# A 16x16 substitution joined by small matmuls, grouped beta/alpha matmuls, and a planner with other costs, in a two-layer hybrid DeltaNet step

## The chip, the core and the metric

The kernel runs on one core of a Trainium2 chip. The metric is the device time in microseconds (us) from start to end of one execution. TensorE (PE in the rows), VectorE (DVE), ScalarE (ACT), GpSimd (POOL) and the DMA queue of SyncE (SP) work side by side. Each works through its own instructions in the program's order, and semaphores tie them together.

## What is computed

128 context tokens and 256 latent tokens (384 in all) pass through two layers. What matters of one layer in the reference:

```python
hn = _rmsnorm(x, norm_g) * (1.0 + scale) + shift
proj = hn @ w_in                 # conv branch, q, k, v, z, beta, alpha, gates
beta = jax.nn.sigmoid(beta_l)    # 16 columns: 8 heads x 2 directions
g = -jnp.exp(a_log) * jax.nn.softplus(alpha_l + dt_bias)
# per head, direction and block of tokens (gated delta rule):
a = jnp.einsum('bhnid,bhnjd->bhnij', kb, k) * decay
a = jnp.where(strict, a, 0.0) + jnp.eye(CHUNK)
u = triangular_solve(a, v * beta)          # unit triangle
w = triangular_solve(a, kb * exp(g))
...
x = x + gate * (merged @ w_o)
```

The triangular solves need the inverse of a unit triangular matrix for each head, direction and block. A head has two directions and three blocks of 128 tokens, so six matrices of 128x128; there are 8 heads in each of 2 layers, 16 heads in all.

## The kernel before

Channels lie on the 128 partitions and the 384 tokens on the free axis. Each weight half of 512 KB comes by a DMA from SP, is rounded by ACT into `whi`, and the rest `wlo` is made by DVE (a few by POOL). An fp32 product is then three matmuls of 384 columns: `whi` with both parts of the activation pair, `wlo` with its first part (`mm3`). A *job* is 48 such matmuls that make one output tile of 128 channels; it runs as four *steps* of 12 (`slot`). In the rows `pm`, `pg` and `px` are PSUM tiles, `t` and `h` are tiles of the pools behind `t1`, `t2` and `h1`.

The order in which instructions are written is made by a planner in the Python code. Each emitted instruction is booked on a clock of its engine (`book`, with costs from `mm_`, `act`, `vec`, `dma`). Side work is written as generators (`spawn`): a `yield` asks to go on after the next step, a `yield "p"` asks to go on when the TensorE clock has passed the time at which the operands are booked. After every step `fill` writes pieces of the 31-tap convolution (`conv31`, on DVE, read from `px`) until the DVE clock has caught up with TensorE's.

In each layer 40 jobs make the conv branch inputs and k, q and v of the heads, five jobs a head. Then come the z jobs, the gates, the merges and the output projection. The heads' side work runs beside these 40 jobs and a dozen after them.

`invert` makes the inverse of a head's six matrices. It takes the 32x32 diagonal blocks (24 of them), sends them through DRAM (`dd`) so that each block lies on one partition of `ax`, and substitutes row by row on POOL: for each of 31 columns an outer product `o` and a subtraction. The result goes through DRAM (`dx`) back to `xc` on 128 partitions. Then small matmuls join 32x32 blocks to 64x64 (`ypf`, `ypb`, then `xf`, `xb`) and 64x64 to 128x128 (`y2p`, `x2p`). `head_out` uses the inverse `U` and runs the scan.

`ba_mm` makes beta and alpha: for each of 16 input tiles one fp32 matmul of 32 output channels and 384 columns, written to the PSUM partitions `32*(k%4)` on. In layer 0 these stand among the matmuls of the modulation (`mod_job`, operand `csil`), in layer 1 between the first steps.

Of the kernel before, what the change touches and what calls it, by code (L numbers as in the profile page):

```python
# [52 lines left out]
for _n, _w in PAR:  # L53
# [3 lines left out]

CST = [("ident", 128), ("mask_f", 128), ("mask_b", 128), ("xmask", 64),
       ("ones", 128), ("sel32", 32), ("sel2", 2)]
# [9 lines left out]
def hybrid_step_kernel(ctx: ExitStack, tc: tile.TileContext, x_in, cvec, w_mod, w_modt, w_first, w_in, w_ba,  # L69
# [63 lines left out]
    def act(out, in_, func, **k):  # L133
# [3 lines left out]
        return nc.scalar.activation(out, in_, func, **k)  # L137

    def mm_(out, lhsT, rhs, start, stop):
# [281 lines left out]
    def mod_job(l, cs):  # L421
# [21 lines left out]
        def finish(v):  # L443
# [14 lines left out]
            while "v" not in rs_x:  # L458
                yield
            h = make_hn(l, k)  # L460
            live[0] += 1 - (k % 2)
            yield "p"
            ba_mm(k, h)
            hn_done.add(k)
# [163 lines left out]
    def make_hn(l, k, lo_eng=ptt):  # L628
# [11 lines left out]
        split(hn[k], h, False, lo_eng)  # L640
        return h
# [171 lines left out]
    def invert(l, hd):  # L813
# [8 lines left out]
        yield  # L822
        dd = dram.tile([P, NI, 32], F32, tag="dd", name="dd", bufs=2)
        dma(out=dd, in_=dg.rearrange("p d b i -> p (d b) i"))
        yield 2
        ax = sub.tile([4 * NI, 32, 32], F32, tag="ax", name="ax", bufs=NA)
        for q in range(4):
            dma(out=ax[NI * q:NI * q + NI], in_=dd[32 * q:32 * q + 32].rearrange("j n i -> n j i"))
        pset(out=ax.rearrange("p i j -> p (i j)")[:, 0:1024:33], value=1.0)
        for j in range(31):  # L830
            n, m = 31 - j, j + 1
            o = sub.tile([4 * NI, 256], F32, tag="o", name="o", bufs=1)
            ov = o[:, 0:n * m].rearrange("p (r c) -> p r c", r=n)
            ptt(out=ov, in0=ax[:, j, j + 1:32].unsqueeze(2).to_broadcast([4 * NI, n, m]),
                                    in1=ax[:, j, 0:m].unsqueeze(1).to_broadcast([4 * NI, n, m]), op=ALU.mult)
            ptt(out=ax[:, j + 1:32, 0:m], in0=ax[:, j + 1:32, 0:m], in1=ov, op=ALU.subtract)
        dx = dram.tile([4 * NI, 32, 32], F32, tag="dx", name="dx", bufs=2)
        dma(out=dx, in_=ax, q="pool")
# [10 lines left out]
        vset(out=U[1][0:64, :, 64:128], value=0.0)  # L849
        xc = t1([P, NI, 32])  # L850
        for q in range(4):
            dma(out=xc[32 * q:32 * q + 32], in_=dx[NI * q:NI * q + NI].rearrange("n i c -> i n c"))
        yield 2
        x64, xt64 = h1([P, NI, 64]), h1([P, NI, 64])
        tt(out=x64.rearrange("p n (e c) -> p n e c", e=2), in0=xc.unsqueeze(2).to_broadcast([P, NI, 2, 32]),
           in1=C("xmask").rearrange("p (e c) -> p e c", e=2).unsqueeze(1).to_broadcast([P, NI, 2, 32]), op=ALU.mult)
# [169 lines left out]
    def layer(l):  # L1026
# [246 lines left out]

        hk = {}

        def open_layer():
            del rs_x["v"]
            yield from rows_task()
            for a in range(HNA):
                hk[a] = make_hn(l, a, tt)  # L1280
            st["open"] = True


        def first_half(i):
            def run(hs, at):
                if i == 0:
                    st["acc"] = [pm(), pm(), pm(), pg([P, NTOK])]
                for q in range(2):
# [3 lines left out]
                    else:  # L1292
                        settle(lambda: "open" in st)
                        if k + HNA < KT:
                            hk[k + HNA] = make_hn(l, k + HNA)

                    def mms(k=k, q=q, h=hk.pop(k) if l else None):
                        if l:
                            ba_mm(k, h)
                        for n in range(4):  # L1300
                            mm3(st["acc"][n], hs[0], 4 * q + n, hn[k], k == 0, k == KT - 1)
# [225 lines left out]
def _consts():  # L1527
# [9 lines left out]
    q, e, cc = i[:, None] // 32, np.arange(64)[None] // 32, np.arange(64)[None] % 32  # L1537
    put("xmask", (e == q % 2) & (cc <= i[:, None] % 32))
    put("mask_f", np.where(i[:, None] <= i[None, :], 0.0, NEG))
# [91 lines left out]
```

## Time and profile before

| what | before |
|---|---|
| median of 3 runs | 2449.17 us (2448.19 to 2454.17) |
| the profiled execution | 2447.77 us, span of its instructions 2446.0 us |
| PE busy | 2330.2 us (95%) |
| DVE busy | 1835.7 us (75%) |
| ACT busy | 951.6 us (39%) |
| POOL busy | 869.1 us (36%) |
| granted TensorE clock, mean | 0.984 |

A share is an average over stages. Matmuls are pipelined, so a row's mean duration of one matmul is longer than the distance between two starts; the distance between starts is what a matmul costs.

### The profile page before, as it was taken

The numbers are of one execution on the slowest core, as the hardware profiler recorded it, in microseconds if no ns is written. First come the engines' busy times: TensorE is split into PE (matmuls) and PEld (weight loads), VectorE is DVE, ScalarE is ACT, GpSimd is POOL, SyncE is SP. The second block draws the span as 40 slices with busy tenths as digits, with TensorE's granted clock in tenths as the row PEclk, the third lists the DMA queues.
The fourth block names the chain that finished last, engine by engine and source line by source line (L and its number), as shares of the span: only waits on it lengthen the run. The fifth ranks groups of instructions, "written<-read, shape, count | busy, mean of one in ns | idle before, by whom it ended". The sixth has DMA issues, their size and how long they took to land.

```text
span 2446.0 us, 40033 instructions
## 1 busy us (share of the span) xinstructions
PE 2330.2 (95%) x14727; PEld 2237.6 (91%) x14727; DVE 1835.7 (75%) x4223; ACT 951.6 (39%) x1823; POOL 869.1 (36%) x1192
## 2 busy tenths in 40 slices
PE   6999989989989999999999999999989999999997
PEld 4789988989979999999998998988889999999997
DVE  3447989989875599899977999999975489333533
ACT  4224444444454222223344444444454322222432
POOL 1120688667630111111242188756670011110212
PEclk9999999999999999999999999999999999999998
DMA  9874433333323688787853433333333477333443
GB/s 340 287 257 149 137 107 99 111 104 104 98 91 109 206 269 265 255 266 259 310 160 104 130 114 108 108 104 113 95 103 114 152 254 239 130 125 132 137 158 111
DMA packets 163269, 398.26 MB, mean 163 GB/s; under 512 B 40960, under 2 KB 70752, under 8 KB 163072
## 3 DMA queue, kind: packets, MB, share of 16 engines
q1 hardware_dynamic: 159376, 387.66, 48.9%
q0 software_dynamic: 2176, 5.90, 0.7%
q8 instruction: 116, 1.90, 0.3%
q10 hardware_dynamic: 1520, 2.13, 0.2%
q14 instruction: 81, 0.66, 0.1%
HBM read 379.72 MB, written 15.91 MB: 162 GB/s over the span
## 4 chain that ended last, share of the span: by engine, by line
PE 64%; DVE 19%; POOL 7%; DMA 3%; issue 3%; ACT 3%; SPq 1%; DVEq 0%; ACTq 0%; POOLq 0%
PE pm L148 54%; DVE t L177 10%; PE pg L148 8%; DVE wlo L177 4%; POOL ax L177 4%; POOL o L177 3%; ACT t L137 2%; DVE h L177 1%; DMA t<-in_w_mod_dram 1%; PE px L148 1%; ACT jk L137 1%; DVE rk0t L177 1%; PE pg L152 1%; SPq L201 1%; DMA w<-in_w_in_dram 1%
## 5 line engine op out<-in xcount | busy, mean ns | idle before, releaser
L148 PE MATMUL pm<-t,whi 128*128 128x384 f32 x7264 | 1903.6, 343 | 5.8 <-ACT whi L137 5.8
L148 PEld LDWEIGHTS pm<-t,whi 128*128 128x128 f32 x7264 | 1314.5, 190 | 26.8 <-ACT whi L137 7.4
L148 PE MATMUL pm<-t,wlo 128*128 128x384 f32 x3632 | 1232.6, 339 | 31.1 <-DVE wlo L177 31.1
L177 DVE TENSOR_TENSOR wlo<-w,whi 128x1024 fp32r<-128x1024 f32 x453 | 587.5, 1298 | 207.3 <-ACT whi L137 206.2
L148 PEld LDWEIGHTS pm<-t,wlo 128*128 128x128 f32 x3632 | 688.2, 189 | 38.1 <-DVE wlo L177 37.9
L137 ACT ACTIVATE whi<-w 128x1024 fp32r<-128x1024 f32 x480 | 505.2, 1054 | 383.0 <-PE pm L148 301.1
L177 POOL TENSOR_TENSOR ax<-ax,o 24x31 f32<-24x31 f32 (+15 forms) x496 | 332.4, 670 | 38.9
L137 ACT ACTIVATE t<-t 128x384 f32<-128x384 f32 (+5 forms) x299 | 137.7, 467 | 525.4 <-DVE t L177 479.9
L177 POOL TENSOR_TENSOR o<-ax 24x31 f32<-24x31 f32 (+15 forms) x496 | 309.4, 624 | 38.9
L177 DVE SCALAR_TENSOR_TENSOR t<-px,par,t 128x113 f32<-128x113 f32 (+26 forms) x768 | 248.7, 367 | 12.0 <-ACT px L137 6.9
L177 POOL TENSOR_TENSOR t<-t,t 128x384 fp32r<-128x384 f32 (+2 forms) x66 | 88.0, 1337 | 383.0 <-DVE t L177 305.4
L177 POOL TENSOR_TENSOR wlo<-w,whi 128x1024 fp32r<-128x1024 f32 x27 | 65.0, 2408 | 433.0 <-ACT whi L137 421.1
L177 DVE SCALAR_TENSOR_TENSOR px<-wm,pg 128x512 f32<-128x512 f32 x256 | 177.1, 692 | 8.7 <-DMA wm<-in_w_modt_dram 5.3
L177 DVE SCALAR_TENSOR_TENSOR wm<-wm,pg 128x512 f32<-128x512 f32 x256 | 167.2, 681 | 7.3 <-PE pg L152 7.3
L137 ACT ACTIVATE t<-pm 128x384 f32<-128x384 f32 x122 | 56.1, 488 | 176.1 <-PE pm L148 175.9
L148 PE MATMUL pg<-t,whi 128*128 128x384 f32 (+1 forms) x416 | 110.9, 348 | 3.3 <-ACT h L137 1.2
L189 POOL MEMSET ax<- 24x32 f32 x16 | 2.5, 158 | 270.7 <-DMA ax<-dd 270.7
L177 DVE TENSOR_TENSOR t<-t,t 128x384 f32<-128x384 f32 (+1 forms) x122 | 81.6, 679 | 22.1 <-ACT t L137 20.9
L177 DVE SCALAR_TENSOR_TENSOR t<-t,t 128x384 f32<-128x384 f32 x96 | 60.0, 625 | 44.1 <-ACT t L137 43.8
L177 POOL TENSOR_TENSOR accx<-accx,t 128x384 f32<-128x384 f32 x28 | 29.6, 1057 | 174.9 <-ACT t L137 146.9
L148 PEld LDWEIGHTS pg<-t,whi 128*128 128x128 f32 x416 | 74.9, 191 | 12.9 <-issue 4.5
L177 POOL TENSOR_TENSOR h<-h,t 128x384 f32<-128x384 f32 x16 | 16.3, 1017 | 172.4 <-DVE t L177 172.4
(152 smaller groups left out, 1683.3 us busy)
## 6 DMA issues: line engine op xcount, KB each, us to landing
w<-in_w_in_dram SPq DMA_DIRECT2D x318, 512.0 KB
wm<-in_w_modt_dram SPq DMA_DIRECT2D x128, 512.0 KB
w<-in_w_p_dram SPq DMA_DIRECT2D x64, 512.0 KB
w<-in_w_o_dram SPq DMA_DIRECT2D x64, 512.0 KB
t<-in_w_mod_dram SPq DMA_DIRECT2D x80, 384.0 KB
w<-in_w_first_dram SPq DMA_DIRECT2D x16, 512.0 KB
t<-in_x_dram SPq DMA_DIRECT2D x16, 384.0 KB
t<-gdram SPq DMA_DIRECT2D x16, 384.0 KB
```

What stands on the lines that cost most here:

```text
L137: return nc.scalar.activation(out, in_, func, **k)
L148: return nc.tensor.matmul(out, lhsT, rhs, start=start, stop=stop)
L152: nc.tensor.transpose(out, in_, ident)
L177: return f(**k)
L189: pset = vec(lambda out, value: nc.gpsimd.memset(out, value), 1e-3, "pool", 0.05)
L201: eng.dma_start(out=out, in_=in_)
```

## The change

Three things are changed together.

1. `invert` substitutes 16x16 blocks: 48 blocks on 48 partitions and 15 columns in place of 24 blocks on 24 partitions and 31 columns. Two instructions (one on ACT, one on DVE) pick the 16x16 blocks before the transfer. Two new stages of 24 small matmuls each (32 rows by 32 columns, 16 columns moving) join pairs of 16x16 to 32x32 between the transfer and the stage at 64. Around them stand a multiply with a mask, a transpose, a memset, two copies out of PSUM and an update on DVE or ACT. The transfers of a head go from ten DMAs to four.
2. `ba_mm` works on four input tiles at once: eight matmuls in a row, four with the first parts of the pairs and four with the second parts.
3. The planner's costs change: a main matmul is booked with (n+32)/2400 us in place of n/2400+0.005, small matmuls by their shape with 0.1 for a change of shape, POOL with a larger base, and a DMA issue with 0.35 us in place of 0.05.

The core of the diff:

```diff
     def mm_(out, lhsT, rhs, start, stop):
         n = size(rhs)
+        rows_, cols = lhsT.shape[0], size(lhsT)
         if rhs.dtype == F32R:
-            c = n / 2400.0 + 0.005
+            c = (n + 32) / 2400.0
+        elif rows_ == 128 and cols == 128:
+            c = max(n, 120) / 600.0 + 0.01
+        elif rows_ == 128:
+            c = n / 2400.0 + 0.01
         else:
-            c = max(n, size(lhsT)) / 600.0 * (0.75 if lhsT.shape[0] < 128 else 1.0)
-            if lhsT.shape[0] == 128 and size(lhsT) == 32:
-                c /= 4
+            c = 0.03 if rows_ == 32 else 0.05
+        shape = (rows_, cols > 32, cols > 64)
+        if shape != array[0]:
+            c += 0.1
+            array[0] = shape
...
-    ptt = vec(nc.gpsimd.tensor_tensor, 2.2e-3, "pool", 0.1)
+    ptt = vec(nc.gpsimd.tensor_tensor, 2.1e-3, "pool", 0.25)
...
-        book(q, 1.0 if q == "pool" else 0.05, [out], [in_], fin - t + 2.0)
+        book(q, 1.0 if q == "pool" else 0.35, [out], [in_], fin - t + 2.0)
...
-    def ba_mm(k, h):
-        g = 32 * (k % 4)
-        mm_(ba["ps"][g:g + 32, :], ba["w"][:, k, :], h, start=(k < 4), stop=(k >= 12))
+    def ba_mm(k):
+        if k % 4 < 3:
+            return
+        for half in range(2):
+            for i in range(k - 3, k + 1):
+                g = 32 * (i % 4)
+                mm_(ba["ps"][g:g + 32, :], ba["w"][:, i, :], hn[i][:, half, :].bitcast(F32),
+                    start=(i < 4 and half == 0), stop=(i >= 12 and half == 1))
...
-        dma(out=dd, in_=dg.rearrange("p d b i -> p (d b) i"))
+        dc, df = t1([P, NI, 16]), dg.rearrange("p d b i -> p (d b) i")
+        act(dc, df[:, :, 0:16], AF.Copy, scale=C("hsel")[:, 0:1])
+        stt(out=dc, in0=df[:, :, 16:32], scalar=C("hsel")[:, 1:2], in1=dc, op0=ALU.mult, op1=ALU.add)
+        dma(out=dd.rearrange("n p j -> p n j"), in_=dc)
...
-        for q in range(4):
-            dma(out=ax[NI * q:NI * q + NI], in_=dd[32 * q:32 * q + 32].rearrange("j n i -> n j i"))
-        for j in range(31):
-            n, m = 31 - j, j + 1
+        dma(out=ax, in_=dd.rearrange("n (g i) j -> (n g) i j", g=8))
+        for j in range(15):
+            n, m = 15 - j, j + 1
...
+        xy = h1([P, 2, NI, 32])
+        x32, y32 = xy[:, 0], xy[:, 1]
+        tt(out=x32 ..., in0=xc ..., in1=C("hmask") ..., op=ALU.mult)
+        vtrans(out=xt32, in_=x32)
+        vset(out=y32[:, NF:, 0:16], value=0.0)
+        yield "p"
+        ypf, ypb = pg([P, NF, 16]), pg([P, NF, 16])
+        for n in range(NF):
+            for q in range(4):
+                g = diag(q)
+                mm_(ypf[g, n, :], ap[0][g, n, 0, g], x32[g, n, 0:16], start=True, stop=True)
+            for q in range(4):
+                g = diag(q)
+                mm_(ypb[g, n, :], ap[1][g, n, 0, g], xt32[g, NF + n, 16:32], start=True, stop=True)
+        yield
+        vcopy(out=y32[:, 0:NF, 0:16], in_=ypf)
+        act(y32[:, NF:, 16:32], ypb, AF.Copy)
+        yield "p"
+        xp = pg([P, NI, 16])
...
+        yield
+        stt(out=x32[:, :, 0:16], in0=xp, scalar=C("lowneg"), in1=x32[:, :, 0:16], op0=ALU.mult, op1=ALU.add)
```

How the instructions stand now is seen in the order of the built programs (rows with an engine's source line, the operation, what it writes and reads, and the shape).

TensorE at the start of layer 1, before: `px` is the beta/alpha sum, and one matmul of it stands ahead of each input tile's twelve main matmuls.

```order
L148 MATMUL px<-t_13471,t_13467 32x384
L148 MATMUL pm<-t_13476,whi 128x384 x2
L148 MATMUL pm<-t_13476,wlo 128x384
...
L148 MATMUL px<-t_13480,t_13467 32x384
L148 MATMUL pm<-t_13485,whi 128x384 x2
```

After, at the fourth input tile of layer 1:

```order
L157 MATMUL pg<-t_13668,wlo 128x384
L157 MATMUL px<-t_13556,t_13547 32x384
L157 MATMUL px<-t_13565,t_13547 32x384
L157 MATMUL px<-t_13668,t_13547 32x384
L157 MATMUL px<-t_13692,t_13547 32x384
...
L157 MATMUL pm<-t_13692,whi 128x384 x2
```

The same four follow once more with the second parts, so eight stand together, which write the four strips of 32 PSUM partitions in turn; there are four such places in each layer in place of sixteen single matmuls.

TensorE at the first head of layer 0, after: the two new stages (`32x16`), a step of twelve main matmuls between them, of which the last row is shown. Each stage has its two rows three times.

```order
L157 MATMUL pm<-t_1625,wlo 128x384
L157 MATMUL pg<-h_3074,t_2438 32x16 x4
L157 MATMUL pg<-t_3075,t_2439 32x16 x4
...
L157 MATMUL pm<-t_590,wlo 128x384
L157 MATMUL pg<-h_3074,t_3075 32x16 x4
L157 MATMUL pg<-h_3074 32x16 x4
```

Before, the first small matmuls at this place are those of the stage at 64 (`pg<-h_3374,t_2421 64x32`), which follow one step after the second new stage now. Counted in jobs of 48 main matmuls from the start of the program, the first of these stages at 64 in layer 0 stand at 25.5, 29.0, 33.0, 36.8, 42.0, 47.0, 52.0 and 57.5 before, and at 23.5, 25.8, 30.8, 35.8, 40.8, 45.8, 51.0 and 57.0 after: one head every five jobs.

DVE at one head of layer 0, after: from the product with the new mask to the transpose that the stage at 64 reads, with the convolution's pieces (`px,par`) between.

```order
L186 TENSOR_TENSOR h_5819<-t_5730,cst 128x192
L186 STREAM_TRANSPOSE t_5820<-h_5819 128x192
...
L186 TENSOR_TENSOR wlo<-w_5654,whi 128x1024
L186 COPY h_5819<-pg 128x3x16
L186 TENSOR_TENSOR wlo<-w_5692,whi 128x1024
L186 SCALAR_TENSOR_TENSOR t_5298<-px,par_93,t_5298 128x119
...
L186 SCALAR_TENSOR_TENSOR t_5298<-px,par_93,t_5298 128x117
L186 SCALAR_TENSOR_TENSOR h_5819<-pg,cst,h_5819 128x6x16
L186 TENSOR_TENSOR h_5967<-h_5819,cst 128x384
L186 STREAM_TRANSPOSE h_5968<-h_5967 128x384
```

Before, the last two of these rows alone stood there (`h_5990<-t_5935,cst` and its transpose), straight behind one `wlo`. The sum over the convolution's outputs (`lnsum` read by TensorE) stands at job 53.0 of layer 0 before and at 50.5 after, so the same convolution pieces are written in fewer steps.

## Rows read from the trace of the kernel before

**Rows 1.** The page: span, busy time by engine, POOL's share in 40 slices.

```profile
span 2446.0 us, 40033 instructions
PE 2330.2 (95%) x14727; PEld 2237.6 (91%) x14727; DVE 1835.7 (75%) x4223; ACT 951.6 (39%) x1823; POOL 869.1 (36%) x1192
...
POOL 1120688667630111111242188756670011110212
```

**Rows 2.** Windows: length, busy and count by engine, granted clock, DMA share, GB/s.

```profile
0.00:140.00 140.00, 116.28 (x866) 86.79 (x867) 58.75 (x131) 49.63 (x92) 19.45 (x19) 0.96 0.91 313
...
290.00:725.00 435.00, 392.96 (x2766) 374.60 (x2765) 388.17 (x968) 197.35 (x473) 296.80 (x472) 0.97 0.33 102
...
1270.00:1360.00 90.00, 89.68 (x467) 75.25 (x466) 69.13 (x148) 41.81 (x90) 26.17 (x20) 1.00 0.36 115
1360.00:1850.00 490.00, 457.91 (x3191) 438.20 (x3190) 448.02 (x1111) 228.82 (x539) 327.26 (x512) 0.97 0.35 108
```

**Rows 3.** Waits of TensorE from 290 to 725 us: total, times, longest.

```profile
PE pm L148 <- DVE wlo L177: 15.2, 7, 7.8
PE pg L148 <- DVE h L177: 9.5, 10, 5.9
```

**Rows 4.** Timeline of TensorE, layer 0's start: start, length, instruction, shape, count.

```profile
47.22 0.34 PE L148 MATMUL pg<-t,wlo 128*128 128x384 f32 x1
47.49 0.83 PE L148 MATMUL px<-t,t 128*32 128x384 f32 x2
48.25 0.61 PE L148 MATMUL pg<-t,whi 128*128 128x384 f32 x2
...
52.35 0.33 PE L148 MATMUL pg<-t,wlo 128*128 128x384 f32 x1
52.61 1.93 PE L148 MATMUL pg<-t,csil 128*32 128x256 f32 x32
54.48 0.45 PE L148 MATMUL pg<-t,whi 128*128 128x384 f32 x1
```

**Rows 5.** Timeline of TensorE at one stage at 64 of layer 0.

```profile
524.20 0.34 PE L148 MATMUL pm<-t,wlo 128*128 128x384 f32 x1
...
524.73 0.34 PE L148 MATMUL pm<-t,wlo 128*128 128x384 f32 x1
524.99 0.55 PE L148 MATMUL pg<-h,t 32*64 32x32 f32 x24
525.47 0.62 PE L148 MATMUL pm<-t,whi 128*128 128x384 f32 x2
```

**Rows 6.** POOL's groups: two of the page, one by shape (300 to 700 us).

```profile
L177 POOL TENSOR_TENSOR ax<-ax,o 24x31 f32<-24x31 f32 (+15 forms) x496 | 332.4, 670 | 38.9
L177 POOL TENSOR_TENSOR o<-ax 24x31 f32<-24x31 f32 (+15 forms) x496 | 309.4, 624 | 38.9
...
L177 POOL TENSOR_TENSOR o<-ax 24x60 f32<-24x60 f32 x15 | 6.9, 459 | 1.2
```

**Rows 7.** DVE's groups by shape, 300 to 700 us: busy, mean ns, idle before.

```profile
L177 DVE TENSOR_TENSOR wlo<-w,whi 128x1024 fp32r<-128x1024 f32 x64 | 87.0, 1362 | 0.6 <-ACT whi L137 0.2
L177 DVE SCALAR_TENSOR_TENSOR t<-t,G,cst 128x128 f32<-128x128 f32 x36 | 19.2, 585 | 0.0
...
L177 DVE TENSOR_TENSOR t<-t,t 128x384 f32<-128x384 f32 x15 | 12.1, 806 | 2.5 <-ACT t L137 2.2
L177 DVE SCALAR_TENSOR_TENSOR t<-pm,par,t 128x127 f32<-128x127 f32 x32 | 10.7, 335 | 0.3 <-ACT t L137 0.2
```

**Rows 8.** DVE's groups by shape, 730 to 1000 us.

```profile
L177 DVE TENSOR_TENSOR wlo<-w,whi 128x1024 fp32r<-128x1024 f32 x57 | 70.8, 1242 | 18.2 <-ACT whi L137 18.1
...
L177 DVE TENSOR_TENSOR t<-t,t 128x384 f32<-128x384 f32 x7 | 3.9, 558 | 0.2
```

**Rows 9.** Timelines of TensorE and of SP's queue near 355 us.

```profile
359.51 0.42 PE L148 MATMUL pg<-h,t 32*64 32x32 f32 x2 [5.87 <-DVE h L177]
...
355.69 1.78 SPq L201 DMA_DIRECT2D t<-dx  x4
```

More of the change, by code (lines that the diff above doesn't have):

```diff
@@ L56 @@
 NPAR = _o
-CST = [("ident", 128), ("mask_f", 128), ("mask_b", 128), ("xmask", 64),
+CST = [("ident", 128), ("mask_f", 128), ("mask_b", 128), ("xmask", 64), ("hmask", 32), ("lowneg", 1), ("hsel", 2),
        ("ones", 128), ("sel32", 32), ("sel2", 2)]
@@ L459, in finish @@
                 yield
-            h = make_hn(l, k)
+            make_hn(l, k)
             live[0] += 1 - (k % 2)
             yield "p"
-            ba_mm(k, h)
+            ba_mm(k)
             hn_done.add(k)
@@ L849, in invert, with diag @@
         vset(out=U[1][0:64, :, 64:128], value=0.0)
-        xc = t1([P, NI, 32])
-        for q in range(4):
-            dma(out=xc[32 * q:32 * q + 32], in_=dx[NI * q:NI * q + NI].rearrange("n i c -> i n c"))
+        xc = t1([P, NI, 16])
+        dma(out=xc, in_=dx.rearrange("(n g) i c -> (g i) n c", g=8))
         yield 2
+        xy = h1([P, 2, NI, 32])
+        x32, y32 = xy[:, 0], xy[:, 1]
+        xt32 = t1([P, NI, 32])
+        tt(out=x32.rearrange("p n (e c) -> p n e c", e=2), in0=xc.unsqueeze(2).to_broadcast([P, NI, 2, 16]),
+           in1=C("hmask").rearrange("p (e c) -> p e c", e=2).unsqueeze(1).to_broadcast([P, NI, 2, 16]), op=ALU.mult)
+        vtrans(out=xt32, in_=x32)
+        vset(out=y32[:, NF:, 0:16], value=0.0)
+        yield "p"
+        def diag(q):
+            return slice(32 * q, 32 * q + 32)
+        ypf, ypb = pg([P, NF, 16]), pg([P, NF, 16])
[11 more added lines that the diff above has]
+        xp = pg([P, NI, 16])
+        for n in range(NF):
+            for q in range(4):
+                g = diag(q)
+                mm_(xp[g, n, :], xt32[g, n, :], y32[g, n, 0:16], start=True, stop=True)
+            for q in range(4):
+                g = diag(q)
+                mm_(xp[g, NF + n, :], y32[g, NF + n, :], x32[g, NF + n, 0:16], start=True, stop=True)
+        yield
+        stt(out=x32[:, :, 0:16], in0=xp, scalar=C("lowneg"), in1=x32[:, :, 0:16], op0=ALU.mult, op1=ALU.add)
         x64, xt64 = h1([P, NI, 64]), h1([P, NI, 64])
-        tt(out=x64.rearrange("p n (e c) -> p n e c", e=2), in0=xc.unsqueeze(2).to_broadcast([P, NI, 2, 32]),
+        tt(out=x64.rearrange("p n (e c) -> p n e c", e=2), in0=x32.unsqueeze(2).to_broadcast([P, NI, 2, 32]),
            in1=C("xmask").rearrange("p (e c) -> p e c", e=2).unsqueeze(1).to_broadcast([P, NI, 2, 32]), op=ALU.mult)
@@ L1279, in open_layer @@
             for a in range(HNA):
-                hk[a] = make_hn(l, a, tt)
+                make_hn(l, a, tt)
             st["open"] = True
@@ L1294, in run, with mms @@
                         if k + HNA < KT:
-                            hk[k + HNA] = make_hn(l, k + HNA)
-                    def mms(k=k, q=q, h=hk.pop(k) if l else None):
+                            make_hn(l, k + HNA)
+                    def mms(k=k, q=q):
                         if l:
-                            ba_mm(k, h)
+                            ba_mm(k)
                         for n in range(4):
@@ L1537, in _consts @@
     q, e, cc = i[:, None] // 32, np.arange(64)[None] // 32, np.arange(64)[None] % 32
-    put("xmask", (e == q % 2) & (cc <= i[:, None] % 32))
+    put("xmask", e == q % 2)
+    e, cc = np.arange(32)[None] // 16, np.arange(32)[None] % 16
+    put("hmask", (e == i[:, None] // 16 % 2) & (cc <= i[:, None] % 16))
+    put("lowneg", -1.0 * (i[:, None] % 32 >= 16))
+    put("hsel", np.arange(2)[None] == i[:, None] // 16 % 2)
     put("mask_f", np.where(i[:, None] <= i[None, :], 0.0, NEG))
```

20 lines of the change are left out of this document (10 added, 10 removed).

## The prediction

> **What bounds the kernel now.** I read the page first. TensorE is busy for 95% of the span and DVE for 75%; POOL's digits show that it works in two long blocks of time, and is nearly idle otherwise [rows 1]. The windows say what lies under these averages [rows 2]. Outside the two blocks TensorE is simply full: from 1270 to 1360 us it is busy for 89.68 of 90 us. In the blocks, 290 to 725 us and 1360 to 1850 us, where the heads run, two engines are near full at once. TensorE is busy for 392.96 of 435 us and 457.91 of 490 us, DVE for 388.17 and 448.02. So TensorE stands idle for 42.0 and 32.1 us, 74 us in all, and behind that its granted clock is 0.97 on average there (1.00 in the window before), which is 0.03 x (435 + 490) = 28 us of full speed. The blocks thus hold some 102 us above the bare work of TensorE, and nothing else in the program holds as much. That is the only large thing that this change can win.
>
> What does TensorE wait for there? In the first block 15.2 us for `wlo`, the rest of a weight that DVE makes, once for 7.8 us, and 9.5 us for `h`, the operands of the inverse that DVE makes [rows 3]. The longest wait of the second sort shows its origin [rows 9]: TensorE waits 5.87 us until 359.51 for the stage at 64; the DMAs that bring the substituted blocks back (`t<-dx`) were issued at 355.69 only. POOL had not finished. POOL's two groups of the substitution are 332.4 + 309.4 = 641.8 us [rows 6], 40.1 us for each of 16 heads, and the heads follow each other at 4 to 5 jobs, so POOL is the longest link of a head's chain.
>
> **What the change removes and adds.** The sum is made against the profiled execution, 2447.8 us, which is 1.4 us below the median of the runs. What the parts cost on TensorE is the distance between starts.
>
> *Beta/alpha.* Three main matmuls start between 524.20 and 524.73 us [rows 5], so one costs 0.53 / 3 = 0.175 us or little more. The matmul of 32 channels alone: the main matmul ahead of it starts at 47.22 and the one behind at 48.25, so it costs 1.03 - 0.175 = 0.86 us [rows 4], and 32 of them 27.5 us. For eight in a row, which write four strips in turn, the nearest row is the modulation: the same form (128 rows by 32 columns), 16 matmuls of 256 columns, four strips in turn, from 52.35 to 54.48, that is 2.13 - 0.175 = 1.96 us [rows 4]. By columns that is 1.96 x (8 x 384)/(16 x 256) = 1.47 us for a group of eight. Layer 1 pays 4 x 1.47 = 5.9 in place of 13.8: -7.9 us, in a window where TensorE is full. Layer 0 could save as much, but there DMA is at 0.91 with 313 GB/s while TensorE idles for 24 of 140 us [rows 2]: the modulation weights may be late next. I take half, -4. Sum -12 us, with bounds of -16 and -8. If the strips did not overlap, a group would cost 8 x 0.86 and the part would be +27; the row on the modulation speaks against it, and I keep that as a rival.
>
> *The two joining stages.* The trace has no 32x32 by 16 matmul. The nearest row is the stage at 64 with 12 matmuls (24 records, 32 rows by 64 columns, 32 columns moving): from 524.73 to 525.47, less 0.175, is 0.57 us [rows 5]. A new stage has twice as many matmuls, each with half the columns on both sides. If columns count, it costs 0.57; if instructions count, 1.14. I take the middle, 0.85, since that stage has a part that does not grow with either. Two stages in 16 heads: 32 x 0.85 = +27 us, from +18 to +36. It lies on the path, since TensorE is what the blocks are short of.
>
> Which end is nearer? The row holds 24 records within 0.55 us, at most 23 ns from one to the next [rows 5]. A rule of the Trainium skill, "TensorE: Matmul & The Clock Gate", section "Wait — 56ns, not 53.3ns?", speaks against this part: the distance between two starts never falls below about 25 ns, however few columns move. By it the 48 records of a new stage would take 1.2 us, the 32 stages some 40 us, and the sum below would be 13 us higher. The row can't tell a floor just under it from work that takes so long; that instructions alone set the price is therefore among the rivals, at the row's 1.14 us.
>
> *DVE and POOL.* POOL's part of a head falls from 62 instructions to 30, none over 64 elements. At the 0.459 us of 60 elements [rows 6] that is 13.8 us in place of 40.1. On DVE six or seven small instructions come to a head (a selection, a product with the mask, a transpose, a memset, a copy, an update). At 0.335 us for about 128 columns [rows 7] they are 1.7 to 2.3 us, +27 to +37 us in all. ACT gains two small ones; it idles enough. Something is given back: where POOL is idle, DVE makes a `wlo` in 1242 ns and a sum of 384 columns in 558 [rows 8]; beside POOL they take 1362 and 806 [rows 7]. The subtraction of 128 columns with both operands in SBUF takes 585 there against 335 for one that reads PSUM [rows 7]. The excess of these three alone is 64 x 0.12 + 15 x 0.25 + 36 x 0.25 = 20.4 us in 400 us with seven heads, 2.9 us a head; with small groups like them I estimate 4. POOL's work falls by two thirds, so 2.7 us a head comes back: 43 us. DVE's load is thus about the same or some 10 us lower, and its long stretches of slow small instructions ahead of a `wlo` get shorter.
>
> *The order.* The planner's step of twelve main matmuls was booked at 12 x 0.165 = 1.98 us and is now at 12 x 0.1733 = 2.08; the trace has 2.10. POOL's 40 us were booked at some 30. With both near the truth, what comes back from POOL should be there when TensorE reaches it, and the heads stand one every five jobs with a step between any two stages. Two stages more also mean 32 more places where DVE must answer within a step: behind the second stage three DVE instructions stand in a row, at most about 1.5 us, in a step of 2.1. That fits only if DVE is not behind.
>
> *Waits.* Of the 102 us I expect half to go, -47: most of what is due to late substitution (11 us in `h`), a part of the `wlo` waits, and the clock that falls behind such waits. Bounds: 0, since DVE stays near full, and -90.
>
> Sum: 2447.8 - 12 + 27 - 47 = 2415.8. The four DMAs in place of ten are priced at nothing: their issue lies on SP, which idles for most of the time behind `wlo`. If the smaller pieces landed later, the stage after them would wait as at 359.51 [rows 9].
>
> **Rivals.**
>
> *Waits nearly vanish.* If DVE gets clearly ahead, TensorE keeps only its work: 2447.8 - 12 + 27 - 90 = 2373. For it: POOL's share falls from 68% to a quarter in the blocks. Against it: DVE was at 89 and 91% and stays close to it. The mechanism is that POOL holds up DVE instructions with two SBUF operands: if each of them lost half a POOL instruction, some 0.32 us [rows 6], and not 0.12 as the `wlo` show, the excess would be over 1 us a job, and far more would come back than I count. Of the short instructions the rows show 0.25 us, of the long one less. The Trainium skill is on this side: "SBUF — State Buffer", section "SBUF: two separate sides", says that such an instruction and a POOL instruction that reads SBUF exclude each other, each for its whole length.
>
> *DVE falls behind (the other side).* The convolution's pieces now end at job 50.5 and not 53.0, so DVE has them, and seven heads' additions, in 2.5 jobs less. The place is the first six heads of each layer. If what POOL gives back is under the 27 us that DVE gets, DVE is the bound there, waits for `wlo` take the place of those that go, and nothing of the 102 us is won: 2447.8 - 12 + 27 = 2463. It decides once DVE is above some 95% of the blocks.
>
> *Gains and costs cancel.* Only the waits for late substitution go, some 15 to 20 us: 2447.8 - 12 + 27 - 18 = 2445.
>
> *Instructions set the price of the new stages.* For it: nothing in the row excludes 23 ns a record. Against it: half the columns on both sides. Then 32 x 1.14 = +36 in place of +27: 2425. The skill's page named above is on this side.
>
> *The strips don't overlap.* +27 in place of -12: 2455.
>
> **How the numbers follow.** About 0.3% (7 us) is what a measurement of this kernel can tell from no change, so faster means under 2442. Chances: the forecast 0.43 (2397 to 2437), waits nearly gone 0.17 (2365 to 2397), the price by instructions 0.07, cancel 0.16, DVE behind 0.14, strips 0.03. Faster is 0.43 + 0.17 + 0.07 = 0.67, same 0.16 + 0.02, slower 0.15. The range leaves out half of the lowest case and some of the highest: 2385 to 2464.
>
> **What would show it.** Right: POOL's substitution near 14 us a head; `px` rows in groups that cost about 1.5 us; the new stages at 0.6 to 1.1 us; `wlo` near 1.25 us in the blocks; TensorE idle for under 45 us in both blocks with a clock of 0.98 or more. Wrong: waits for `wlo` over 30 us in all; DVE above 95% in the blocks; waits for the modulation weights beyond the first; a stage of 24 small matmuls above 1.2 us.

## The result, and the profile after

The changed kernel takes 2394.68 us (median of 4 runs, 2392.92 to 2397.25); the kernel before, beside it on the same chip, 2449.33 (4 runs, 2448.19 to 2454.17). The ratio is 0.9774, with a 95% interval of 0.9757 to 0.9791: 55 us faster. The forecast was 2416, with a range of 2385 to 2464. The time is in the range and on the forecast's side, but below the likeliest case's own span (2397 to 2437): it is in that of the rival "waits nearly vanish".

The page of the changed kernel, profiled in its run of 2397.25 us, answers to [rows 1] and [rows 6]:

```profile
PE 2318.9 (97%) x16327; PEld 2237.7 (93%) x16327; DVE 1760.3 (73%) x4319; ACT 957.7 (40%) x1855; POOL 395.7 (17%) x680
...
POOL 0120311111200011012333121122010101110212
...
L186 POOL TENSOR_TENSOR o<-ax 48x15 f32<-48x15 f32 (+7 forms) x240 | 83.5, 348 | 18.9
L186 POOL TENSOR_TENSOR ax<-ax,o 48x15 f32<-48x15 f32 (+7 forms) x240 | 82.6, 344 | 18.8
```

POOL's two blocks are gone. DVE has 96 instructions more and is busy for 75 us less.

To say where the time went I cut both executions at the same work. One job is 48 main matmuls; the stretches below are jobs 0 to 13 (layer 0's beta/alpha), 23 to 64 (layer 0's heads), 64 to 120 (the long run of `w` with the pieces of the modulation between), 120 to 126 (layer 1's beta/alpha) and 130 to 178 (layer 1's heads). Windows of the kernel before, cut so: start:end, length, busy (and count) of PE, PEld, DVE, ACT and POOL, granted clock, DMA share, GB/s.

```profile
26.20:196.60 170.40, 165.50 (x1195) 133.44 (x1195) 74.39 (x155) 53.69 (x92) 32.52 (x34) 0.98 0.84 283
...
288.70:779.90 491.20, 449.16 (x3151) 429.84 (x3150) 420.22 (x1026) 223.93 (x525) 298.10 (x473) 0.97 0.34 104
779.90:1253.90 474.00, 474.00 (x2721) 473.52 (x2721) 418.80 (x991) 152.24 (x197) 78.43 (x55) 1.00 0.75 250
1253.90:1321.50 67.60, 67.60 (x337) 53.56 (x336) 46.98 (x75) 31.13 (x60) 28.66 (x22) 1.00 0.42 128
...
1358.70:1902.30 543.60, 511.51 (x3511) 491.76 (x3510) 476.94 (x1162) 252.55 (x585) 327.26 (x512) 0.97 0.36 109
```

And of the changed kernel:

```profile
25.90:191.30 165.40, 158.31 (x1228) 135.22 (x1229) 74.99 (x155) 53.76 (x92) 33.41 (x34) 0.99 0.85 294
...
283.50:742.80 459.30, 448.84 (x3872) 430.50 (x3871) 383.48 (x1061) 227.26 (x539) 74.25 (x215) 0.99 0.34 108
742.80:1230.60 487.80, 479.10 (x2721) 474.18 (x2720) 417.64 (x991) 150.66 (x197) 80.62 (x55) 1.00 0.74 244
1230.60:1296.50 65.90, 62.65 (x370) 53.74 (x369) 46.69 (x73) 31.17 (x60) 28.48 (x22) 1.00 0.35 118
...
1333.70:1853.00 519.30, 508.26 (x4279) 489.10 (x4278) 440.73 (x1214) 257.01 (x600) 88.19 (x256) 1.00 0.36 111
```

Read the lengths first: -5.0, -31.9, **+13.8**, -1.7 and -24.3 us, in all -49.1 of the -50.5 between the two profiled runs. The two blocks with the heads give 56.2 us, and the stretch between them, which the change was not about, takes a quarter of that back.

Then read the blocks (23 to 64 and 130 to 178) across. TensorE's idle time is length less busy: 42.0 + 32.1 before, 10.5 + 11.0 after, so 52.6 us less. The granted clock is at half of full speed in short stretches; summed over these windows from the trace (the rows above round it to hundredths) it took 27.3 us and now takes 6.8, so 20.5 less. What remains, +17, is by this sum the work that TensorE was given. DVE is the surprise: 897.2 us before, 824.2 after, though the joins added 87 instructions to it there.

[rows 3] has TensorE's waits in the first block alone. Over the whole execution (total, times, longest) they were, before and after:

```profile
PE pm L148 <- DVE wlo L177: 31.1, 21, 7.8
...
PE pg L148 <- DVE h L177: 12.2, 17, 5.9
```

```profile
PE pm L157 <- DVE wlo L186: 15.6, 11, 2.8
PE pg L157 <- DMA t<-in_w_mod_dram: 14.3, 1, 14.3
...
PE pm L157 <- POOL t L186: 3.5, 8, 0.9
PE pg L157 <- DVE h L186: 3.3, 7, 0.6
```

The waits for `h`, in which a late substitution shows, are down from 12.2 to 3.3 us, none over 0.6. The one for the modulation weights was there before too (14.0 us). The wait of `pm` for POOL's `t` is new.

Two places on TensorE's timeline carry the terms that the prediction had to bound. One group of eight beta/alpha matmuls:

```profile
91.94 0.34 PE L157 MATMUL pg<-t,wlo 128*128 128x384 f32 x1
92.21 1.50 PE L157 MATMUL px<-t,t 128*32 128x384 f32 x16
93.64 0.62 PE L157 MATMUL pm<-t,whi 128*128 128x384 f32 x2
```

From 91.94 to 93.64, less 0.175 for the main matmul, the group costs 1.53 us (forecast 1.47, from [rows 4]). This is in layer 0, where the four groups cost 1.42 to 1.53 us. In layer 1 each of the four costs 1.95 to 1.97:

```profile
1256.41 0.34 PE L157 MATMUL pg<-t,wlo 128*128 128x384 f32 x1
1256.68 1.93 PE L157 MATMUL px<-t,t 128*32 128x384 f32 x16
1258.54 0.61 PE L157 MATMUL pm<-t,whi 128*128 128x384 f32 x2
```

Why the same eight matmuls take longer there is open. And one new joining stage:

```profile
282.66 0.34 PE L157 MATMUL pm<-t,wlo 128*128 128x384 f32 x1
282.93 0.25 PE L157 MATMUL pg<-h,t 32*32 32x16 f32 x8
...
283.46 0.62 PE L157 MATMUL pm<-t,whi 128*128 128x384 f32 x2
```

It costs 0.80 - 0.175 = 0.62 us, near the lower bound of 0.57, so columns count and not instructions. Of the 32 stages two, one in each layer, also hold a wait of 2.7 us for ACT's `vk`. The 48 records of a stage (two for each of 24 matmuls) follow each other within 13 ns on average. The floor of about 25 ns between two starts that the Trainium skill states ("TensorE: Matmul & The Clock Gate", section "Wait — 56ns, not 53.3ns?") does not hold for these small matmuls; by it the stage would have taken 1.2 us, as an estimate.

Last, DVE's groups in the first block of the changed kernel, by shape (busy, mean ns, idle before):

```profile
L186 DVE TENSOR_TENSOR wlo<-w,whi 128x1024 fp32r<-128x1024 f32 x83 | 101.6, 1224 | 6.0 <-ACT whi L137 5.9
...
L186 DVE TENSOR_TENSOR t<-t,t 128x384 f32<-128x384 f32 x30 | 16.8, 560 | 1.4 <-ACT t L137 0.9
...
L186 DVE SCALAR_TENSOR_TENSOR t<-t,G,cst 128x128 f32<-128x128 f32 x36 | 10.2, 338 | 0.0
...
L186 DVE TENSOR_TENSOR rk0t<-sk,rk 128x3 f32<-128x3 f32 x12 | 1.9, 161 | 0.4
```

The first three took 1362, 806 and 585 ns beside POOL in the window of [rows 7] (over all of these jobs 1335, 680 and 585); the first two are now at what [rows 8] show where POOL idles, 1242 and 558. The same instruction on the same data is up to 1.7 times as fast. Even the tiny last one, of three columns, took nearly twice as long in the kernel before:

```profile
L177 DVE TENSOR_TENSOR rk0t<-sk,rk 128x3 f32<-128x3 f32 x12 | 3.6, 296 | 0.4
```

Not every instruction of DVE was slow beside POOL: a piece of the convolution, which reads PSUM, takes 335 ns for 128x120 before and 336 after. And it is not only those with two SBUF operands: `cq<-ss`, which multiplies three columns by a constant, took 526 ns and takes 163.

### The profile page after: what moved, and what is told of

Its sections match the earlier page's. It is cut to its first block, busy times and chain, and to the rows that moved or that the text cites. A ratio compares the mean times of both kernels' runs of the same rounds, so it can differ in the third digit from the quotient of the medians.

```text
span 2395.4 us, 42732 instructions
## 1 busy us (share of the span) xinstructions
PE 2318.9 (97%) x16327; PEld 2237.7 (93%) x16327; DVE 1760.3 (73%) x4319; ACT 957.7 (40%) x1855; POOL 395.7 (17%) x680
## 4 chain that ended last, share of the span: by engine, by line
PE 42%; DVE 6%; ACT 2%; issue 1%; POOL 0%; DVEq 0%; ACTq 0%
PE pm L157 37%; DVE t L186 4%; PE pg L157 4%; ACT t L137 1%; DVE wlo L186 1%; PE pg L161 1%; ACT jk L137 0%; ACT whi L137 0%; POOL t L186 0%; DVE h L186 0%; DVE rk0t L186 0%; DVE lnsum L186 0%; POOL wlo L186 0%; DVE rk L186 0%; PE px L157 0%
## 5 line engine op out<-in xcount | busy, mean ns | idle before, releaser
L186 DVE TENSOR_TENSOR wlo<-w,whi 128x1024 fp32r<-128x1024 f32 x453 | 568.8, 1256 | 218.6 <-ACT whi L137 215.0
L186 DVE SCALAR_TENSOR_TENSOR t<-px,par,t 128x113 f32<-128x113 f32 (+26 forms) x768 | 247.5, 367 | 10.4 <-ACT px L137 5.3
L186 DVE SCALAR_TENSOR_TENSOR t<-t,t 128x384 f32<-128x384 f32 x96 | 53.4, 557 | 49.9 <-ACT t L137 49.4
L186 DVE TENSOR_TENSOR t<-t,t 128x384 f32<-128x384 f32 (+1 forms) x122 | 72.3, 603 | 23.5 <-ACT t L137 22.2
L186 POOL TENSOR_TENSOR o<-ax 48x15 f32<-48x15 f32 (+7 forms) x240 | 83.5, 348 | 18.9
L186 POOL TENSOR_TENSOR ax<-ax,o 48x15 f32<-48x15 f32 (+7 forms) x240 | 82.6, 344 | 18.8
L157 PE MATMUL pg<-t,wlo 128*128 128x384 f32 (+1 forms) x208 | 71.2, 342 | 0.0
L186 DVE SCALAR_TENSOR_TENSOR t<-t,pm 128x384 f32<-128x384 f32 x64 | 35.2, 551 | 40.2 <-PE pm L157 39.8
```

The costliest lines, as they stand in the source:

```text
L186: return f(**k)
```

## The experiments

Two theories stood against each other: that the shorter substitution gives the gain, by what POOL no longer does to DVE and by being in time; and that the order made by the new costs gives it. The first four runs take the change apart.

**The new costs alone.** The kernel before, with the planner's new prices and nothing else:

```diff
-            c = n / 2400.0 + 0.005
+            c = (n + 32) / 2400.0
...
-    ptt = vec(nc.gpsimd.tensor_tensor, 2.2e-3, "pool", 0.1)
+    ptt = vec(nc.gpsimd.tensor_tensor, 2.1e-3, "pool", 0.25)
...
-        book(q, 1.0 if q == "pool" else 0.05, [out], [in_], fin - t + 2.0)
+        book(q, 1.0 if q == "pool" else 0.35, [out], [in_], fin - t + 2.0)
```

> The kernel before with the planner's three new costs alone (main and small matmuls, POOL, DMA issue); 32x32 substitution and single beta/alpha matmuls stay. Theory A (the shorter substitution makes the gain, the costs only let it be used): 2440 to 2455 us, TensorE idle in the two blocks still 55 us or more, since POOL is still busy for 40 us a head. Theory B (the order makes the gain): 2405 to 2430 us, idle in the blocks under 45 us.

Measured: 2469.24 us against 2448.57, ratio 1.0078 (1.0059 to 1.0097): slower by some 19 us, above the ranges of both theories. Its windows of jobs 23 to 64, 64 to 120 and 130 to 178:

```profile
287.30:777.00 489.70, 450.95 (x3150) 431.75 (x3150) 418.23 (x1020) 224.31 (x525) 299.63 (x474) 0.96 0.33 105
777.00:1265.30 488.30, 478.90 (x2723) 474.14 (x2722) 417.32 (x991) 150.77 (x197) 81.49 (x55) 1.00 0.73 244
...
1370.10:1925.70 555.60, 517.30 (x3511) 497.29 (x3510) 477.01 (x1165) 253.28 (x584) 325.79 (x512) 0.95 0.33 106
```

The blocks gain nothing (-1.5 and +12.0 us; theory A had not foreseen the loss), and DVE's load there is as before. The +14 in the middle is there too, so it comes from the prices and not from the substitution. The theory that the order gives the gain falls.

**The parts of the new form with the old costs.** Three kernels: the joined substitution alone, the grouped beta/alpha alone, and both together.

```diff
-        ax = sub.tile([4 * NI, 32, 32], F32, tag="ax", name="ax", bufs=NA)
+        NS = 8 * NI
+        ax = sub.tile([NS, 16, 16], F32, tag="ax", name="ax", bufs=NA)
...
-            ba_mm(k, h)
+            ba_mm(k)
```

> The 16x16 substitution with its two joining stages alone; planner's costs and beta/alpha as before. Theory A: 2400 to 2420 us, wlo near 1225 ns in the blocks, TensorE idle in the blocks 40 us or less. Theory B: 2430 to 2455 us, since an order made by the old costs still puts stages where their operands are late.

Measured: 2407.89 us against 2448.57, ratio 0.9837 (0.9809 to 0.9865), 40 us faster.

> The grouped beta/alpha matmuls alone. If only the work of TensorE counts: -13 us, 2436 us (27.5 us of single matmuls become 8 groups of 1.5 to 1.9 us). If the making of the activation pairs is next in line in layer 1 and the modulation weights in layer 0, as waits of 0.4 to 0.9 us for POOL in the changed kernel suggest: -3 to -8 us, 2441 to 2446 us.

Measured: 2435.70 us, ratio 0.9942 (0.9923 to 0.9961), 14 us faster. The total is what the work of TensorE alone would give, but it is not made up so: layer 0's stretch gives 4.1 us, jobs 120 to 126 take 65.9 us in place of 67.6, and 3.2 and 3.6 us come from the blocks, where nothing of the beta/alpha matmuls runs. Executions of one kernel differ by as much as these last two.

> The changed kernel with the planner's old costs. Theory A: 2390 to 2405 us, at most 10 us above the changed kernel or even below it, since the new costs also put more of the fill work into a step in the modulation stretch, where 8.7 us of waits for wlo are new. Theory B: 2420 us or more.

Measured: 2397.43 us, ratio 0.9785 (0.9768 to 0.9803). The interval overlaps that of the whole change (0.9757 to 0.9791). The two parts multiply: 0.9837 x 0.9942 = 0.9780. So the new form gives the whole gain. Where the prices act is seen in the windows of jobs 23 to 64, 64 to 120 and 130 to 178 with the old ones:

```profile
286.70:749.20 462.50, 449.48 (x3802) 431.71 (x3798) 383.11 (x1061) 227.59 (x538) 76.02 (x211) 0.98 0.34 107
749.20:1223.30 474.10, 473.99 (x2721) 473.34 (x2721) 417.80 (x991) 152.10 (x197) 79.06 (x55) 1.00 0.75 250
...
1327.70:1852.40 524.70, 510.75 (x4279) 491.26 (x4279) 438.84 (x1207) 257.38 (x601) 95.42 (x256) 0.99 0.35 110
```

With the new form the new prices give 3.2 + 5.4 = 8.6 us in the blocks and lose 13.7 between them.

**POOL's load put back, behind the substitution.** To tell whether POOL slows DVE, the next kernels give POOL products whose results nobody reads; the rest of the computation is left as it is. They stand behind each head's substitution, so I expected no head to be late. One kernel has long products, one short ones:

```diff
-            o = sub.tile([NS, 64], F32, tag="o", name="o", bufs=1)
+            o = sub.tile([NS, 220], F32, tag="o", name="o", bufs=1)
...
+        for _ in range(36):
+            nc.gpsimd.tensor_tensor(out=o[0:24, 0:220], in0=cst[0:24, 0:220], in1=cst[0:24, 256:476], op=ALU.mult)
```

```diff
+        for _ in range(75):
+            nc.gpsimd.tensor_tensor(out=o[0:48, 0:56], in0=cst[0:48, 0:56], in1=cst[0:48, 256:312], op=ALU.mult)
```

> The changed kernel in the same order on all other engines, with 36 extra POOL products of 24x220 elements behind each head's transfer out of POOL (results unused), so POOL is again busy for some 40 us a head but the substitution itself is not later. If POOL holds up DVE instructions with two SBUF operands: wlo in the blocks back at 1300 ns or more, t<-t,G,cst at 500 or more, TensorE idle in the blocks 20 us or more above the changed kernel, time 2415 to 2440 us. If the late substitution was what cost: within 5 us of the changed kernel, 2390 to 2400 us.

> The same with 75 extra POOL products of 48x56 elements in place of 36 of 24x220, which should take about as long. If the share of time in which POOL works is what counts: like the run with the long ones. If only long POOL instructions hold DVE (in the changed kernel wlo took 1220 ns even beside the short ones): within 5 us of the changed kernel, wlo near 1225 ns.

Measured: 2515.80 us with the long products (ratio 1.0271, 1.0257 to 1.0285) and 2449.39 with the short ones (0.9996, 0.9987 to 1.0005), the long ones above their range and the short ones in neither of theirs. The premise failed. The waits of TensorE for `h` in the kernel with short products:

```profile
PE pg L157 <- DVE h L186: 38.0, 15, 16.4
```

Two waits of over 16 us, and of 7.7 and 8.9 in the kernel with long products: the second head of each layer follows the first so closely that its substitution stood behind the added work. Both kernels mix lateness with contention and settle neither. What they do show is the price of lateness: two late heads are 32.5 us of idle TensorE.

**The same, without lateness.** No products behind the first head of a layer, and 60 in place of 75 short ones:

```diff
-        for _ in range(36):
+        for _ in range(36 if hd["h"] else 0):
...
-        for _ in range(75):
+        for _ in range(60 if hd["h"] else 0):
```

> As the run with 36 long extra POOL products a head, but none behind each layer's first head, whose successor follows within 45 us: there the extra work had made the substitution of the second head late (waits of 7.7 and 8.9 us for h), which was not meant. Now only the load on POOL is left. If long POOL instructions hold up DVE and DVE then TensorE: wlo still over 1300 ns in most of the blocks, TensorE idle in the blocks still 30 us or more above the changed kernel, time 2460 to 2500 us. If lateness was the larger part: 2400 to 2425 us.

Measured: 2496.99 us against 2451.47, ratio 1.0188 (1.0174 to 1.0202): about 100 us above the changed kernel. The waits for `h` are 5.8 us in all, none over 1.3, so this is not lateness; those for `wlo` are 73.2 us. Its two blocks, and in the first the same groups of DVE; the last fence is POOL's added group in the whole execution:

```profile
283.60:790.70 507.10, 460.31 (x3879) 439.69 (x3871) 435.68 (x1061) 227.51 (x539) 282.69 (x467) 0.95 0.31 97
...
1379.40:1952.50 573.10, 526.89 (x4280) 505.85 (x4279) 495.11 (x1214) 257.62 (x600) 295.20 (x508) 0.95 0.32 101
```

```profile
L186 DVE TENSOR_TENSOR wlo<-w,whi 128x1024 fp32r<-128x1024 f32 x83 | 110.1, 1327 | 5.2 <-ACT whi L137 5.1
...
L186 DVE SCALAR_TENSOR_TENSOR t<-t,G,cst 128x128 f32<-128x128 f32 x36 | 21.2, 640 | 0.0
...
L186 DVE TENSOR_TENSOR rk0t<-sk,rk 128x3 f32<-128x3 f32 x12 | 4.0, 336 | 0.4
```

```profile
L858 POOL TENSOR_TENSOR o<-cst 24x220 f32<-24x220 f32 x504 | 413.5, 820 | 38.7
```

DVE executes the same 1061 instructions and needs 435.7 us in place of 383.5; in both blocks it is busy for 930.8 us in place of 824.2. The durations of the kernel before are back, and a little more.

> The same with 60 short extra products (48x56) for each head but the first of a layer. In the earlier run with short ones two waits for h were 16 us each and DVE was hardly slower. If short POOL instructions don't hold DVE: no wait for h above 2 us, wlo under 1250 ns and 2395 to 2410 us. If a busy POOL counts whatever its instructions: as the long ones.

Measured: 2412.78 us, ratio 0.9845 (0.9827 to 0.9862): some 17 us above the changed kernel, just beyond the range for "don't hold". No wait for `h` is over 0.6 us. Its two blocks, and the same groups:

```profile
280.40:748.70 468.30, 451.86 (x3876) 432.98 (x3871) 392.27 (x1061) 227.56 (x539) 251.48 (x635) 0.98 0.33 106
...
1337.80:1866.20 528.40, 512.14 (x4278) 492.47 (x4278) 449.34 (x1214) 257.15 (x600) 265.50 (x676) 0.99 0.34 109
```

```profile
L186 DVE TENSOR_TENSOR wlo<-w,whi 128x1024 fp32r<-128x1024 f32 x83 | 103.5, 1247 | 6.0 <-ACT whi L137 5.8
...
L186 DVE SCALAR_TENSOR_TENSOR t<-t,G,cst 128x128 f32<-128x128 f32 x36 | 12.9, 410 | 0.0
...
L186 DVE TENSOR_TENSOR rk0t<-sk,rk 128x3 f32<-128x3 f32 x12 | 1.9, 162 | 0.4
```

```profile
L858 POOL TENSOR_TENSOR o<-cst 48x56 f32<-48x56 f32 x840 | 353.0, 420 | 64.9
```

POOL is busy for 54% of the first block, against 56% with the long products. Yet DVE's load in both blocks grows by 17.4 us only (to 841.6), not by 106.6. It is not the share of time in which POOL is busy that decides, but what its instructions are like.

The kernel before bears out that their length matters. Its substitution has instructions of 31 to 256 elements, and the 84 `t<-t,G,cst` of its two blocks can be sorted by the longest one that runs beside each: 344 ns beside none (12 of them), 317 up to 64 elements (6), 499 from 65 to 128 (4), 592 from 129 to 192 (23) and 678 above (39). Two things are not told apart by the runs. A long product also works on more elements: the 504 long ones on 2.4 times as many per partition as the 840 short ones, against 6 times the loss. And the means of 820 and 420 ns hold POOL's own waits: the medians are 655 and 299 ns.

**Length or partitions?** The long products have 24 partitions, the short ones 48. The last run puts the short ones on 24:

```diff
-            nc.gpsimd.tensor_tensor(out=o[0:48, 0:56], in0=cst[0:48, 0:56], in1=cst[0:48, 256:312], op=ALU.mult)
+            nc.gpsimd.tensor_tensor(out=o[0:24, 0:56], in0=cst[0:24, 0:56], in1=cst[0:24, 256:312], op=ALU.mult)
```

> As the run with 60 short extra products behind each head but the first, on 24 partitions in place of 48 (the long ones ran on 24). If the length of a POOL instruction decides whether DVE is held: like the run on 48 partitions, 2405 to 2418 us, t<-t,G,cst under 400 ns. If the number of partitions decides: towards the long ones, above 2440 us.

Measured: 2412.89 us against 2449.99, ratio 0.9847 (0.9831 to 0.9864), the same; the products take 417 ns and `t<-t,G,cst` 407, a little above the 400 expected. The number of partitions makes no difference, so what is left is the length of an instruction, or its elements per partition, which go together here.

**The loss between the blocks.** In jobs 64 to 120 the planner fills DVE with pieces of the modulation (`px<-wm,pg` and `wm<-wm,pg`). It books a piece at 0.069 + 512 x 0.00104 = 0.60 us. I took this for too little, since the rows have 0.69 us for the product and 0.08 or 0.14 for the reading of its accumulator. But these durations overlap. On the changed kernel's timeline a product, the reading behind it, and the next product:

```profile
901.28 0.68 DVE L186 SCALAR_TENSOR_TENSOR wm<-wm,pg 128x512 f32<-128x512 f32 x1
901.89 0.08 DVE L186 DVE_READ_ACCUMULATOR wm<-wm,pg 128x1 f32 x1
901.89 0.68 DVE L186 SCALAR_TENSOR_TENSOR wm<-wm,pg 128x512 f32<-128x512 f32 x1
```

The next product starts 0.61 us behind the first, together with the reading, so a piece takes 0.61 us and the booking is right. Three kernels book more for them: 0.09 more; the same with every second low part of layer 1's pairs moved from POOL to DVE; and 0.06 more with all of these low parts, and some of the raw operands', on DVE. The computation is the same. The cuts are those of the last of the three:

```diff
-            book(e, base + 0.06 * len(row) + max(size(x) for x in [k["out"]] + ins) * rate, outs, ins)
+            book(e, base + 0.06 * len(row) + (0.06 if k.get("accum_out") is not None else 0.0) + max(size(x) for x in [k["out"]] + ins) * rate, outs, ins)
...
-            split(raw[k], h, False, ptt)
+            split(raw[k], h, False, tt if k > 3 else ptt)
...
-                            make_hn(l, k + HNA)
+                            make_hn(l, k + HNA, tt)
```

> The changed kernel with one cost more: a DVE instruction that also sums its row (accum_out) is booked with 0.09 us more, which is the mean of what the trace shows above the plan in the modulation rows. If the new waits for wlo between jobs 64 and 120 come from fill work that is booked too cheaply: those waits (8.7 us) fall under 3 us and the time to 2383 to 2390 us. If not: 2392 to 2397 us.

Measured: 2397.23 us against 2448.99, ratio 0.9780 (0.9767 to 0.9794): no gain over the changed kernel. Its windows of jobs 64 to 120 and 120 to 126:

```profile
744.20:1218.20 474.00, 474.00 (x2721) 473.68 (x2721) 410.65 (x978) 149.56 (x189) 68.76 (x48) 1.00 0.75 251
1218.20:1294.30 76.10, 69.66 (x369) 58.06 (x368) 54.68 (x87) 34.18 (x69) 36.08 (x30) 0.91 0.31 105
```

The 13.8 us came back whole, and 10.2 of them went one stretch further on: POOL now has 36.1 us of work in 76 us, and TensorE idles for 6.4, waits for POOL's `t`, and its granted clock is 0.91 on average. The traces show what differs. Counted in windows of four jobs, the old prices put at most 36 pieces beside TensorE (the kernel before, and the two kernels with the joined substitution and old costs), the new ones up to 38, and these with 0.09 more at most 34. The pieces then end later: 29 are left for jobs 116 to 120, where the changed kernel has none and the old prices leave 8 to 10.

> As the run before, and in layer 1 every second low part of the activation pairs is made by DVE in place of POOL. If the pairs are next in line behind the grouped beta/alpha matmuls: the 3.2 us of waits for POOL between jobs 121 and 126 go, 2 to 4 us below the run before. If DVE is short there: no change or slower.

Measured: 2396.08 us, ratio 0.9778 (0.9764 to 0.9792). Jobs 120 to 126 still take 74.5 us: with half of the low parts off POOL the stretch is hardly shorter, and 28 pieces still stand in jobs 116 to 120.

> The changed kernel with 0.06 us for a row sum in the planner (0.09 took the waits between jobs 64 and 120 away, but then eight operands of the raw jobs came late at job 120), all low parts of layer 1's activation pairs and half of those of the raw operands on DVE. If both places are bound by POOL and by the cost of the row sums: jobs 64 to 126 in 540 to 546 us (changed kernel 554), time 2380 to 2390 us. If DVE is what is short there: 2392 us or more.

Measured: **2385.98 us** (2381.11 to 2387.92) against 2451.47, ratio 0.9736 (0.9723 to 0.9750). The interval lies below that of the changed kernel (0.9757 to 0.9791): this version beats both. Its windows of the same two stretches:

```profile
737.80:1211.80 474.00, 474.00 (x2722) 473.68 (x2721) 416.85 (x990) 152.17 (x197) 71.97 (x51) 1.00 0.75 250
1211.80:1276.30 64.50, 61.35 (x368) 53.40 (x367) 47.14 (x94) 31.37 (x60) 8.16 (x8) 1.00 0.37 126
```

Both are now as good as the best seen, and POOL has 8 us of work where it had 28. As price and engine were changed at once, and the two kernels with 0.09 differ in the price too, their shares are not told apart; with 0.06 only 16 pieces are left for jobs 116 to 120.

## Why the prediction was right, and where it was off

The side was right and the mechanism was the one named, but it came as strongly as in the rival "waits nearly vanish" (chance 0.17) and not as in the forecast's own case (0.43). Terms were mis-sized, one step was wrong and one loss was not foreseen. That the time is in the range is in part luck: without the 13.8 us lost in jobs 64 to 120 it would have been some 2381, below 2385. By term, for the profiled runs:

| term | forecast | measured |
|---|---|---|
| beta/alpha, layer 0 | -4 | -5.0 |
| beta/alpha, layer 1 | -7.9 | -1.7 |
| joining stages and other work of TensorE in the blocks | +27 | +16.9 (32 x 0.62 = 20 for the stages) |
| waits and clock in the blocks | -47 | -73.1 (52.6 idle, 20.5 clock) |
| jobs 64 to 120 | 0 | +13.8 |
| all other stretches | 0 | -1.4 |
| sum | -32 | -50.5 |

**Waits.** "Of the 102 us I expect half to go, -47" is the mis-sized term that decided: 73 went, nearer to its outer bound of -90 than to -47. Its root is one step earlier, "2.7 us a head comes back: 43 us", from which it followed that "DVE's load is thus about the same or some 10 us lower". DVE fell by 73 us in the blocks with some 25 us of instructions added there (a head's six measured 0.35, 0.38, 0.10, 0.20, 0.31 and 0.31 us, 1.65 in all; the forecast's 1.7 to 2.3 was for five to seven at 0.335, and six are 2.0), so it got back 98. Two things were missed. The excess went whole, and not by the two thirds by which POOL's work falls: the three priced groups alone gave back 46 us where 31 were counted. And the small ones, guessed at 1 us a head, gave 35 us where 12 were counted: the row of three columns, 296 ns before and 161 now, stands for 372 instructions of three or six columns in the blocks, which lost 0.1 us each on average. DVE stands at 83% and 85% of the blocks, far from the 95% at which it would have been the bound. (That TensorE "is simply full" outside the blocks was read too widely: [rows 2] has it idle for 24 of the first 140 us, and of these the wait of 14 us for the modulation weights is still there.)

How the gain divides between DVE's relief and the substitution being in time is only in part settled. Contention alone was shown to be worth it: with long products added and no head late, all of the gain and more is gone again. The waits for `h` were 12.2 us in the kernel before, and could give no more than that and the clock behind them; that most of the 73 us is DVE's is argued from this, since no run had the late substitution of the kernel before without its contention.

**Exclusion.** The Trainium skill was on the right side here: "SBUF — State Buffer", section "SBUF: two separate sides", has a DVE instruction with two SBUF operands and a POOL instruction that reads SBUF exclude each other for the whole of an instruction. The runs agree in direction and in that POOL's length counts. They show the same for `cq<-ss`, which has one SBUF operand (631 ns beside the long products, 163 in the changed kernel). In size they don't follow it simply: with POOL busy for the same share and half as long in each instruction (420 and 820 ns), one would estimate half the loss; measured, `t<-t,G,cst` loses 72 ns in place of 302, and `rk0t` 1 in place of 175. Why short instructions hold DVE so little is open; between 56 and 220 elements there are only the sorted instructions of the kernel before.

**The order.** "With both near the truth, what comes back from POOL should be there when TensorE reaches it" was wrong as a reason for a gain. The new prices alone made the kernel before 19 us slower, and with the new form they make no difference that was measured: 8.6 us better in the blocks, 13.7 worse between. Booking 0.09 us more for a piece of the modulation alone brought 474.0 us back there, and so did all the old prices. So what costs is how much of DVE's work the new prices put into a step. That the piece itself was priced too low, as was expected before the run, does not hold: it was booked at 0.60 and takes 0.61. More likely the old price of TensorE's step, 1.98 us where it takes 2.10, had kept a reserve for DVE by chance, and the right one took it away; this is argued, since no run changed TensorE's price alone.

**Beta/alpha.** The price of a group was right in layer 0 (1.53 against 1.47), and there 5.0 us came where 4 were forecast. In layer 1 only 1.7 of the 7.9 us arrived. A group costs 1.96 there, so four save 13.8 - 7.8 = 6 us at most; TensorE's work is shorter by 5.0 (busy 62.65 us in place of 67.60), and it waits for POOL's low parts, next in line, seven times for 3.2 us in all. I asked what would be late next in layer 0, where DMA was near full, and not in layer 1.

**Stages and substitution.** 0.62 us a stage and not 0.85: by columns. (At the prediction's other price of 1.2 us a stage the 32 make 38.4 us, and the sum would have been 11 us higher, not 13.) POOL's part is 166.1 / 16 = 10.4 us a head (13.8 forecast). The four DMAs cost nothing that shows: no wait for `h` is over 0.6 us. Of the rivals, that DVE falls behind, that the strips don't overlap and that instructions set the price are each refuted by these rows.

## What to carry to other kernels

When work leaves an off-path engine that slows the bottleneck's helper, price it by every group of the helper, small ones first: compare the mean of each shape in a stretch where the other engine idles with that beside it, and sum over all. If the work must stay, cut it into short instructions: with POOL over half busy in pieces of 0.42 us DVE lost 17 us in the blocks, in pieces of 0.82 us 107. When a planner's prices are put right, look for the reserve that a wrong one may have kept: here a step was booked longer, up to 38 pieces in place of 36 went beside four jobs, and 14 us were lost there. And take the price of a pipelined instruction from start to start, not from its duration.

## What the runs showed of the hardware that was not expected

- POOL's hold on DVE depends on the length of POOL's instruction (or on its elements per partition, which were not varied apart from it) far more than on its share of time: 128x128 with two SBUF operands takes 338 ns beside an idle POOL, 410 beside instructions of 420 ns and 640 beside instructions of 820 ns.
- The 24 matmuls of a stage, 32x32 by 16, take 0.62 us for their 48 records, 13 ns a record on average.
- Eight matmuls of 32 channels and 384 columns in four strips cost 1.42 to 1.53 us in layer 0 and 1.95 to 1.97 in layer 1 of the same execution.
- A 128x512 product with an accumulator has a second row on DVE, of 82 or 140 ns, but the next product starts together with it, 0.61 us behind the first.
